# An indexed sum of a mixture-of-experts stage issued behind a branch instead of ahead of it

## The chip, the cores and the metric

The kernel runs on one core of one Trainium2 chip, in one launch. The metric is the time of one execution on the device, in microseconds (us); lower is better. The time of the kernel before is the median of three runs. All times below are us of one profiled execution unless they are marked ns, and places in it are told by the us from its start.

## The reference

Two transformer layers run one after the other on 512 tokens of width 1024, all in float32. The change lies in the last part of the second layer, a mixture of 32 experts. Two of the 32 are chosen for each token, and every expert is a small gated network:

```python
def run_block(args):
    xb, e = args
    return (jax.nn.silu(xb @ w_gate[e]) * (xb @ w_up[e])) @ w_down[e]
...
out = jnp.zeros((t, dm), jnp.float32).at[stok].add(y_sorted * sw[:, None])
...
x = x + gate2 * ffn
return rms_norm_2(x, g_final)
```

So the rows of an expert are gathered by index, pass through three products (1024 to 512 twice, 512 to 1024), and are added by index into the residual `x`, which is then normalised.

## The kernel before, in words

The expert stage fills the last third of the kernel, from about 1200 us on. It works through 16 *pairs* of experts, p and p + 16, numbered 0 to 15, with 128 rows a pair. The pair's two experts are e0 and e1.

**Products.** Weights are float32 and come from DRAM by DMA (started by SP, the sync engine). A piece of 128x1024 is a *part*; a *split* (`parts`, L118) writes it as a rounded value, by ScalarE (ACT), and the remainder, by VectorE (DVE). TensorE (PE) then makes three matmuls for each product (L128, L129, L130), so each part feeds six matmuls. A pair has 24 parts. Gate and up products gather in PSUM buffers S. A silu on ACT (L1819) and a `scalar_tensor_tensor` on DVE (L1820) make `h` of them; four transposes on PE (L1832) turn it into a PSUM buffer T; ACT and DVE split that into `hh` (L171). The down product goes to two PSUM buffers G, called `py`, one for each half of the 1024 columns. e0's down product starts in `py`, e1's is added to it. G(p, e0) below is the down product of e0 of pair p.

**The end of a pair.** `scatter` multiplies the two halves of `py` into the tile `y` (L1887, DVE; there is one `y`), and GpSimd (POOL) issues an indirect DMA that adds the rows of `y` into the residual `x2_d` in DRAM (L1888). There are only two buffers G, so the first matmul of G(p + 1, e0) has to wait until `y` of pair p has been made.

**The rows of the next pair.** `rows_in` gathers them into one of two tiles `xg` (L1711, POOL), transposes them in two halves through buffers T (L1726, PE; there are two T, shared with the transposes of `h`), scales them (L1734, three columns by ACT; L1732, one by DVE), and splits them (L1736 `x0` by ACT, L1737 `x1` by POOL).

**The pause.** After pair 6 (MID is 7) `pause` prepares the weights of pair 7, makes splits ahead, and calls `overflow`, which handles pairs with more than 128 rows in a loop under `tc.If(n > 0)` (L1932 loads n, L1933 is the branch). Every engine takes this branch. In this input n is 0, and the body isn't run.

**What sets the order.** The program is written for a scheduler that plans the queues of all engines by its own estimates; each engine then runs its queue strictly in order and waits at semaphores. A statement's place in the code is only one input to that plan. The end of the stage is `sums`, which loads `x2_d` again after the last indexed sum (L1968, waiting for `self.scattered`), and `finish`, which squares these rows (L1986 on ACT, L1989 on POOL), adds the last pair and writes the output.

Of the kernel before, what the change touches and what calls it, by code (L numbers as in the profile page):

```python
# [9 lines left out]
F32 = mybir.dt.float32  # L10
# [13 lines left out]
S, D = 512, 1024  # L24
NE, CAP = 32, 128
MID = 7
# [46 lines left out]
class Kernel:  # L73
# [1797 lines left out]
    def experts(self, h, hn_d, x2_d, loaded):  # L1871
        nc = self.nc
        last = NE // 2 - 1
        with self.pool("mo") as wk:
            first, last_x, there = self.first_rows(x2_d, wk)

            def rest():
                self.rows_scaled(1, h, hn_d, last_x)
                self.router_rest(there, last_x, wk)

            self.later = [4, rest]

            def scatter(py, row):
                y = wk.tile([128, D], F32, name="y", bufs=1)
                for half in range(2):
                    c = slice(half * 512, half * 512 + 512)
                    nc.vector.tensor_mul(y[:, c], py[half], self.g2[:, c])  # L1887
                self.scattered = nc.gpsimd.indirect_dma_start(  # L1888
                    out=x2_d, out_offset=bass.IndirectOffsetOnAxis(ap=row, axis=0), in_=y, in_offset=None,
                    bounds_check=S - 1, oob_is_err=False, compute_op=OP.add)  # L1890

            def pieces(p):
                return self.expert_pieces(p), self.expert_pieces(p + 16)

            def job(p):
                def between(rest):
                    if p < last:
                        return []
                    w, self.xs = self.sums(x2_d, rest)
                    return w  # L1900

                def done(py):
                    if p < last:
                        scatter(py, self.ti[:, p:p + 1])
                    else:
                        self.finish(py, wk)

                there = p == MID + 1
                return (pieces(p), lambda: first if p == 0 else self.rows_in(self.ti[:, p:p + 1], self.xg[p % 2], hn_d, wk, there),
                        [self.tw[:, e, p:p + 1] for e in range(2)], between, done)  # L1910

            def pause():

                self.gather(self.ti[:, MID + 1:MID + 2], self.xg[(MID + 1) % 2], hn_d)
                i = self.nraw % len(self.raws)
                raws, n = [r for r in self.raws[i:] + self.raws[:i] if r not in self.spare], 10
                self.raws, self.nraw, self.nparts = raws, 0, 0
                loaded = [self.load(w) for w in self.in_order(MID)[2:][:n]]
                ready = [self.parts(loaded[i // 2][:, i % 2 * 2:i % 2 * 2 + 2]) for i in range(2)]
                places, nparts = self.w_places, self.nparts  # L1920
                self.raws, self.w_places = self.spare, places[-1:]
                self.overflow(last, pieces, scatter, hn_d, wk)
                self.raws, self.nraw = raws[n:] + self.spare + raws[:n], 0
                self.w_places, self.nparts = places, nparts
                return loaded, ready

            self.pairs([job(p) for p in range(last + 1)], wk, loaded, MID, pause)

    def overflow(self, last, pieces, scatter, hn_d, wk):

        nc, tc = self.nc, self.tc
        n = nc.values_load(self.over[0:1, 0:1], min_val=0, max_val=7)  # L1932
        with tc.If(n > 0):  # L1933
            with tc.For_i(0, n, 1) as i:
                p = nc.values_load(self.over[0:1, bass.ds(i + 8, 1)], min_val=0, max_val=last)
                sl = wk.tile([128, 8], F32, name="osl", bufs=1)
                oj = wk.tile([128, 1], F32, name="oj", bufs=1)
                nc.vector.tensor_copy(oj, self.overj[:, bass.ds(i, 1)])
                nc.vector.tensor_scalar(sl, self.slot, oj, None, op0=OP.subtract)
                ti = wk.tile([128, 16], I32, name="oti", bufs=1)  # L1940
                tw = wk.tile([128, 2, 16], F32, name="otw", bufs=1)
                R = self.xg[MID % 2].bitcast(BF)[:, 0:1024].rearrange("p (i s) -> p i s", i=8)
                self.slot_tokens(sl, ti, R)
                self.slot_weights(tw, R)
                t1 = wk.tile([128, 1], I32, name="ot1", bufs=1)
                w1 = wk.tile([128, 2, 1], F32, name="ow1", bufs=1)
                nc.vector.tensor_copy(t1, ti[:, bass.ds(p, 1)])
                nc.vector.tensor_copy(w1, tw[:, :, bass.ds(p, 1)])
                rows = wk.tile([128, D], F32, name="y", bufs=1)
                self.pairs([(pieces(p), lambda: self.rows_in(t1, rows, hn_d, wk), [w1[:, 0], w1[:, 1]],  # L1950
                             lambda rest: [], lambda py: scatter(py, t1))], wk)

    def sums(self, x2_d, rest):

# [152 lines left out]
```

## Time and profile before

| | |
|---|---|
| median of 3 runs | 1790.49 us (1790.27 to 1791.97) |
| the profiled execution | 1795.8 us |
| its span | 1794.0 us |
| granted TensorE clock, mean | 0.988 of full speed |
| busy: PE, DVE, ACT, POOL | 96%, 77%, 64%, 26% of the span |
| L118 splits on ACT / on DVE | 353.8 + 127.7 us / 421.9 + 151.2 us |
| idle PE put down to the branch of L1933 | 5.2 us |

The profile is one execution, taken apart by engine. A busy share is an average over the span. An instruction's row has its start, its duration, its engine, its line, the tile that it writes and those that it reads, and in brackets the idle time of its engine just before it and what ended that. An engine with a q behind its name is the engine's sequencer, where branches and semaphores are handled. Matmuls overlap, so their durations add up to more than the distance between their starts.

### The profile page before, as it was taken

To read this page: it belongs to the slowest core of one execution; us is meant where nothing else is said; L and a number is where in the kernel's file an instruction comes from. 1 tells how busy PE (TensorE), PEld (TensorE's weight loads), DVE (VectorE), ACT (ScalarE), POOL (GpSimd) and SP (SyncE) were. 2 spreads that over 40 slices of the span, in tenths; PEclk is the share of its full clock that TensorE was granted. 3 is DMA by queue.
4 is the path that set the end of the run, shared out by engine and by line. 5 is a ranking of instruction groups with operands and counts; after the bars stand their busy time and mean duration, and the time that the engine had idled before them with its cause. 6 is when DMAs were issued, how large, how long until landed. Compare 5 with 4: busy or idle time off the path is not lost. (4 is left out here: it accounts for less than half of the span.)

```text
span 1794.0 us, 24961 instructions
## 1 busy us (share of the span) xinstructions
PE 1722.5 (96%) x8996; PEld 1414.4 (79%) x8996; DVE 1385.7 (77%) x2028; ACT 1149.6 (64%) x1814; POOL 461.2 (26%) x428
## 2 busy tenths in 40 slices
PE   6999999998999999999999999979999989999996
PEld 3878977887898888888978888757877767787874
DVE  4758788887687474747756877879999979999997
ACT  4646765764555343435555765568888868888886
POOL 2114326435032333333313300111212112121113
PEclk9999999998999999999999999989999999999998
DMA  9543204217446655554432224669999999999954
GB/s 344 172 130 106 78 30 160 87 60 245 149 152 210 201 184 192 187 188 159 141 95 71 71 67 165 233 203 366 366 360 366 327 323 381 374 367 365 371 209 168
DMA packets 234912, 377.71 MB, mean 211 GB/s; under 512 B 11817, under 2 KB 102565, under 8 KB 234784
## 3 DMA queue, kind: packets, MB, share of 16 engines
q1 hardware_dynamic: 223904, 348.22, 56.5%
q0 software_dynamic: 10880, 27.85, 5.2%
q8 instruction: 72, 1.18, 0.3%
q14 instruction: 56, 0.46, 0.1%
HBM read 366.64 MB, written 20.73 MB: 216 GB/s over the span
## 5 line engine op out<-in xcount | busy, mean ns | idle before, releaser
L118 ACT ACTIVATE w<-raw 128x1024 fp32r<-128x1024 f32 (+2 forms) x350 | 353.8, 1017 | 298.4 <-PE G L129 230.5
L118 DVE TENSOR_TENSOR w<-raw,w 128x1024 fp32r<-128x1024 f32 (+2 forms) x350 | 421.9, 1225 | 115.6 <-ACT w L118 113.8
L128 PE MATMUL G<-u,w 128*128 128x512 f32 (+1 forms) x688 | 265.5, 387 | 3.2 <-DVE mo L1090 1.3
L129 PE MATMUL G<-u,w 128*128 128x512 f32 (+1 forms) x688 | 264.4, 385 | 2.0 <-DVE u L922 1.1
L130 PE MATMUL G<-u,w 128*128 128x512 f32 (+1 forms) x688 | 264.7, 386 | 0.6 <-DVE w L118 0.6
L129 PE MATMUL S<-w,x 128*128 128x512 f32 x504 | 200.9, 399 | 0.8 <-DVE w L118 0.8
L128 PE MATMUL S<-w,x 128*128 128x512 f32 x504 | 196.2, 395 | 5.4 <-PEq L1933 5.2
L130 PE MATMUL S<-w,x 128*128 128x512 f32 x504 | 198.2, 393 | 0.0
L118 DVE TENSOR_TENSOR w<-rawa,w 128x1024 fp32r<-128x1024 f32 x122 | 151.2, 1271 | 15.4 <-ACT w L118 15.3
L128 PEld LDWEIGHTS G<-u,w 128*128 128x128 f32 x688 | 129.8, 189 | 30.4 <-issue 2.8
L129 PEld LDWEIGHTS G<-u,w 128*128 128x128 f32 x688 | 129.8, 189 | 27.9 <-DVE u L922 1.6
L118 ACT ACTIVATE w<-rawa 128x1024 fp32r<-128x1024 f32 x122 | 127.7, 1059 | 36.7 <-PE S L130 23.0
L130 PEld LDWEIGHTS G<-u,w 128*128 128x128 f32 x688 | 129.9, 189 | 26.3 <-DVE w L118 1.8
L406 POOL TENSOR_TENSOR acc<-acc,araw 128x512 f32<-128x512 f32 x60 | 87.6, 1479 | 236.8 <-ACT araw L404 236.6
L128 PEld LDWEIGHTS S<-w,x 128*128 128x128 f32 x504 | 95.7, 190 | 27.2 <-issue 5.7
L129 PE MATMUL G<-hid,w 128*128 128x512 f32 (+1 forms) x320 | 111.1, 347 | 1.2 <-DVE hid L1131 1.2
L129 PEld LDWEIGHTS S<-w,x 128*128 128x128 f32 x504 | 95.7, 190 | 20.3 <-DVE w L118 1.1
L130 PE MATMUL G<-hid,w 128*128 128x512 f32 (+1 forms) x320 | 111.3, 348 | 0.0
L130 PEld LDWEIGHTS S<-w,x 128*128 128x128 f32 x504 | 95.7, 190 | 19.7 <-DVE x L1773 0.3
L128 PE MATMUL G<-hid,w 128*128 128x512 f32 (+1 forms) x320 | 110.8, 347 | 0.0
L129 PE MATMUL G<-w,hh 128*128 128x512 f32 x248 | 100.7, 406 | 2.3 <-DVE w L118 0.9
L1737 POOL TENSOR_TENSOR x<-xg,x 128x512 fp32r<-128x512 f32 x30 | 44.9, 1498 | 218.9 <-ACT x L1736 218.9
(652 smaller groups left out, 4028.8 us busy)
## 6 DMA issues: line engine op xcount, KB each, us to landing
raw<-in_mlp_w_dram SPq DMA_DIRECT2D x36, 1024.0 KB, 5.5
raw<-in_w_in_dram SPq DMA_DIRECT2D x33, 1024.0 KB, 5.4
raw<-in_w_expert_up_dram SPq DMA_DIRECT2D x28, 1024.0 KB, 9.6
raw<-in_w_expert_gate_dram SPq DMA_DIRECT2D x27, 1024.0 KB, 9.2
raw<-in_w_expert_down_dram SPq DMA_DIRECT2D x27, 1024.0 KB, 8.1
araw<-in_w_ada_dram SPq DMA_DIRECT2D x96, 256.0 KB, 3.7
rawa<-in_w_expert_gate_dram SPq DMA_DIRECT2D x21, 1024.0 KB, 9.5
rawa<-in_w_expert_up_dram SPq DMA_DIRECT2D x20, 1024.0 KB, 8.5
```

Source lines behind the costliest of these rows:

```text
L118: ins = nc.scalar.activation(r[0], v, AF.Copy), nc.vector.tensor_sub(r[1], v, r[0])
L128: first = nc.tensor.matmul(ps, lhs[0], rhs[0], start=start, stop=False)
L129: nc.tensor.matmul(ps, lhs[0], rhs[1], start=False, stop=False)
L130: self.behind = nc.tensor.matmul(ps, lhs[1], rhs[0], start=False, stop=stop)
L406: nc.gpsimd.tensor_add(x, x, raw)
L1737: nc.gpsimd.tensor_sub(x[1][:, s], y[:, s], x[0][:, s])
```

## The change

`scatter` gets two arguments. `held` is true for pair 6 alone: then `y` is made as before, but the indexed sum isn't issued; `pause` issues it (`add`) behind the call of `overflow`. `pause` asks for one split ahead of `overflow` rather than two. In the body of the loop the rows go into `self.xg[MID % 2]` rather than a tile `y`, as `y` now holds pair 6's result over the loop. No instruction that runs with n = 0 is added or taken away: 15 indexed sums and 30 halves of `y` are there as before. Lines behind the change move by 1, 8 or 9: L1887 is now L1888, L1888 is L1896, L1933 is L1942, L1968 is L1977, L1986 is L1995.

```diff
-            def scatter(py, row):
-                y = wk.tile([128, D], F32, name="y", bufs=1)
+            def scatter(py, row, y=None, held=False):
+                if y is None:
+                    y = wk.tile([128, D], F32, name="y", bufs=1)
                 for half in range(2):
                     c = slice(half * 512, half * 512 + 512)
-                    nc.vector.tensor_mul(y[:, c], py[half], self.g2[:, c])
+                    ins = nc.vector.tensor_mul(y[:, c], py[half], self.g2[:, c])
+                if held:
+
+                    self.held = y, row
+                else:
+                    add(y, row)
+
+            def add(y, row):
                 self.scattered = nc.gpsimd.indirect_dma_start(
                     out=x2_d, out_offset=bass.IndirectOffsetOnAxis(ap=row, axis=0), in_=y, in_offset=None,
                     bounds_check=S - 1, oob_is_err=False, compute_op=OP.add)
...
                     if p < last:
-                        scatter(py, self.ti[:, p:p + 1])
+                        scatter(py, self.ti[:, p:p + 1], held=p + 1 == MID)
...
-                ready = [self.parts(loaded[i // 2][:, i % 2 * 2:i % 2 * 2 + 2]) for i in range(2)]
+                ready = [self.parts(loaded[0][:, 0:2])]
...
                 self.overflow(last, pieces, scatter, hn_d, wk)
                 self.raws, self.nraw = raws[n:] + self.spare + raws[:n], 0
                 self.w_places, self.nparts = places, nparts
+                add(*self.held)
                 return loaded, ready
...
-                rows = wk.tile([128, D], F32, name="y", bufs=1)
+                rows = self.xg[MID % 2]
                 self.pairs([(pieces(p), lambda: self.rows_in(t1, rows, hn_d, wk), [w1[:, 0], w1[:, 1]],
-                             lambda rest: [], lambda py: scatter(py, t1))], wk)
+                             lambda rest: [], lambda py: scatter(py, t1, rows))], wk)
```

The scheduler's queues differ in more than this. Three places of them follow, before and with the change.

**POOL at the pause.** The rows run from the last split of the rows of pair 7 to the gather of pair 8; the rows left out are the body of the loop. Before:

```order
L1737 TENSOR_TENSOR x_13926<-xg_11557,x_13925 128x512 x2
L1888 DMA x_d<-y,ti 512x1024
L1932 TENSOR_LOAD over
L1933 COMPARE_AND_BRANCH
...
L1933 ISA
L1933 UNCONDITIONAL_BRANCH
L1711 DMA xg_11557<-hn_d,ti 128x1024
```

Now:

```order
L1737 TENSOR_TENSOR x_13926<-xg_11557,x_13925 128x512 x2
L1941 TENSOR_LOAD over
L1942 COMPARE_AND_BRANCH
...
L1942 ISA
L1942 UNCONDITIONAL_BRANCH
L1896 DMA x_d<-y,ti 512x1024
L1711 DMA xg_11557<-hn_d,ti 128x1024
```

The indexed sum of pair 6 stands behind the branch, next to the gather. On PE, ACT, DVE and SP the rows ahead of the branch stand in the order that they had: the second split asked for there (and a third) is still made ahead of the branch.

**DVE around G(14, e0).** The rows `y<-G` are pair 13's result; `hh` and the rows behind it are what G(14, e0) and the rows of pair 15 need. Before:

```order
L1887 TENSOR_TENSOR y<-G,g_11351 128x512
L118 TENSOR_TENSOR w_16706<-raw_16693,w_16705 128x1024
L118 TENSOR_TENSOR w<-raw_16715,w 128x1024
L1887 TENSOR_TENSOR y<-G,g_11351 128x512
...
L118 TENSOR_TENSOR w<-rawa,w 128x1024
L171 TENSOR_TENSOR hh_16788<-T,hh_16787 128x512
L1732 TENSOR_SCALAR xg_11557<-T,gain_11126,mods_131 128x128
L118 TENSOR_TENSOR w_16826<-rawa,w_16825 128x1024
L118 TENSOR_TENSOR w_16839<-rawa,w_16838 128x1024
L118 TENSOR_TENSOR w_16849<-rawa,w_16848 128x1024
L118 TENSOR_TENSOR w<-rawa,w 128x1024
L1732 TENSOR_SCALAR xg_11557<-T,gain_11126,mods_131 128x128
```

Now:

```order
L118 TENSOR_TENSOR w<-rawa,w 128x1024
L171 TENSOR_TENSOR hh_16786<-T,hh_16785 128x512
L1732 TENSOR_SCALAR xg_11557<-T,gain_11126,mods_131 128x128
L118 TENSOR_TENSOR w_16824<-rawa,w_16823 128x1024
L1732 TENSOR_SCALAR xg_11557<-T,gain_11126,mods_131 128x128
L1888 TENSOR_TENSOR y<-G,g_11351 128x512 x2
L118 TENSOR_TENSOR w_16837<-rawa,w_16836 128x1024
```

Both halves of `y` have moved from between the splits of the pair's gate product to a place behind the second `xg`, 17 rows later for the first half. On PE the second four transposes of `xg` (L1726) have moved with it: they stood among the matmuls of G(14, e0) and now stand right ahead of them, and the first row of G(14, e0) now waits for DVE's `y`. On ACT the second three `xg` (L1734) stand right behind the first `x0` (L1736) rather than three splits later. Pair 12's `y`, in front of G(13, e0), has moved in the same way, with two splits rather than one between the two `xg`. Pair 11's two halves stand two rows ahead of the `hh` of G(12, e0), with one split between. The halves of pairs 9 and 10 stand two or three rows later than before, eight rows or more ahead of `hh`; those of pairs 7 and 8 have not moved.

**DVE behind G(14, e1).** `y` is pair 14's result, the last one that goes through an indexed sum; the last row is the `h` of (15, e0). Before:

```order
L118 TENSOR_TENSOR w_17015<-p_17012,w_17014 128x1024
L1887 TENSOR_TENSOR y<-G,g_11351 128x512
L118 TENSOR_TENSOR w_17025<-p_17012,w_17024 128x1024
L118 TENSOR_TENSOR w<-p_17034,w 128x1024
L1887 TENSOR_TENSOR y<-G,g_11351 128x512
L118 TENSOR_TENSOR w_17046<-p_17034,w_17045 128x1024
L118 TENSOR_TENSOR w_17062<-raw_17059,w_17061 128x1024
L118 TENSOR_TENSOR w_17072<-raw_17059,w_17071 128x1024
L118 TENSOR_TENSOR w<-raw_17081,w 128x1024
L1820 SCALAR_TENSOR_TENSOR h<-S,tw,h 128x512
```

Now:

```order
L118 TENSOR_TENSOR w_17013<-p_17010,w_17012 128x1024
L118 TENSOR_TENSOR w_17023<-p_17010,w_17022 128x1024
L118 TENSOR_TENSOR w<-p_17032,w 128x1024
L118 TENSOR_TENSOR w_17044<-p_17032,w_17043 128x1024
L118 TENSOR_TENSOR w_17060<-raw_17057,w_17059 128x1024
L118 TENSOR_TENSOR w_17070<-raw_17057,w_17069 128x1024
L118 TENSOR_TENSOR w<-raw_17079,w 128x1024
L1888 TENSOR_TENSOR y<-G,g_11351 128x512 x2
L1820 SCALAR_TENSOR_TENSOR h<-S,tw,h 128x512
```

The second half, which the indexed sum waits for, has moved behind four more splits. POOL's queue behind it is the same as before: the indexed sum, two weight loads, `g_final`, the four loads of `x2_d`, the last gather. On ACT the first square of `finish` has moved behind the last `hh` (`x`, L171).

## Rows read from the trace of the kernel before

**Rows 1.** Busy time by stretch: stretch, us; PE, PEld, DVE, ACT, POOL; clock; DMA.
```profile
1470.00:1530.00 60.00, 59.44 (x272) 47.31 (x271) 55.80 (x54) 50.74 (x64) 11.91 (x7) 1.00 1.04 382
```

**Rows 2.** Waits from 1470 to 1760: us in total, times, longest us.
```profile
ACT w L118 <- PE S L130: 30.7, 97, 0.5
PEld G L130 <- DVE hh L171: 5.3, 16, 0.4
```

**Rows 3.** Line L1933, the branch: ns shortest/median/longest, start of the first and last.
```profile
L1933 PEldq COMPARE_BRANCH  x1: 7982/7982/7982, 1451.3 to 1451.3; - x1
L1933 ACTq COMPARE_BRANCH  x1: 50/50/50, 1453.7 to 1453.7; - x1
```

**Rows 4.** Order of time, PE, around the pause: start, us, instruction, idle before.
```profile
1454.12 0.40 PE L130 MATMUL G<-w,hh 128*128 128x512 f32 x1
1459.76 0.76 PE L128 MATMUL S<-w,x 128*128 128x512 f32 x1 [5.25 <-PEq L1933]
...
1465.02 0.41 PE L128 MATMUL S<-w,x 128*128 128x512 f32 x1
```

**Rows 5.** Order of time, POOL, around the pause.
```profile
1438.72 1.64 POOL L1737 TENSOR_TENSOR x<-xg,x 128x512 fp32r<-128x512 f32 x1 [4.42 <-ACT x L1736]
1456.89 1.56 POOL L1888 DMA_INDIRECT x_d<-y,ti  x1 [16.52 <-DVEq L1933]
1460.23 1.06 POOL L1711 DMA_INDIRECT xg<-hn_d,ti  x1 [1.77 <-PEq L1933]
```

**Rows 6.** Order of time, DVE, from 1709 to 1732, around G(14, e0).
```profile
1711.46 0.68 DVE L1887 TENSOR_TENSOR y<-G,g 128x512 f32<-128x512 f32 x1
...
1723.61 1.23 DVE L118 TENSOR_TENSOR w<-rawa,w 128x1024 fp32r<-128x1024 f32 x1
1724.75 0.68 DVE L171 TENSOR_TENSOR hh<-T,hh 128x512 fp32r<-128x512 f32 x1
1725.35 0.40 DVE L1732 TENSOR_SCALAR xg<-T,gain,mods 128x128 f32<-128x128 f32 x1
1726.09 1.23 DVE L118 TENSOR_TENSOR w<-rawa,w 128x1024 fp32r<-128x1024 f32 x1 [0.33 <-ACT w L118]
```

**Rows 7.** Order of time, PE, at the start of G(14, e0).
```profile
1724.35 0.40 PE L130 MATMUL S<-w,x 128*128 128x512 f32 x1
...
1724.59 0.39 PE L128 MATMUL G<-w,hh 128*128 128x512 f32 x1
...
1729.10 0.60 PE L1726 MATMUL T<-ident,xg 128*128 128x128 f32 x4
```

**Rows 8.** Order of time, ACT, around G(14, e0).
```profile
1724.98 1.07 ACT L118 ACTIVATE w<-rawa 128x1024 fp32r<-128x1024 f32 x1
1725.93 0.61 ACT L1819 ACTIVATE h<-S 128x512 f32<-128x512 f32 x1
1726.41 0.65 ACT L1736 ACTIVATE x<-xg 128x512 fp32r<-128x512 f32 x1
1726.93 3.21 ACT L118 ACTIVATE w<-rawa 128x1024 fp32r<-128x1024 f32 x3
1730.05 1.14 ACT L1734 ACTIVATE xg<-T,mods,gain 128x128 f32<-128x128 f32 x3
```

**Rows 9.** Order of time, PE, after another idle time, in an earlier stage.
```profile
427.76 0.79 PE L129 MATMUL G<-kT,w 128*128 128x512 f32 x1 [2.29 <-DVE kT L171]
```

**Rows 10.** PE by stretch there: stretch, us; PE busy; clock; DMA share, GB/s.
```profile
428.00:432.00 4.00, 4.00 (x9) 0.50 0.62 204
```

**Rows 11.** Order of time, DVE and POOL, behind pair 14.
```profile
1750.11 0.68 DVE L1887 TENSOR_TENSOR y<-G,g 128x512 f32<-128x512 f32 x1
...
1758.07 2.12 POOL L1968 DMA_DIRECT2D rawa<-x_d  x4 [2.48 <-DMA x_d<-y,ti]
```

**Rows 12.** Order of time, ACT, at the end.
```profile
1768.53 1.06 ACT L1986 ACTIVATE y<-rawa 128x1024 f32<-128x1024 f32 x1 [0.42 <-DMA rawa<-x_d]
...
1776.31 0.30 ACT L205 ACTIVATE ss<-ss,eps 128x4 f32<-128x4 f32 x1
```

## The prediction

> **What bounds the kernel now.** I read busy time by stretch first: which engine is full where the change acts? From 1470 to 1530, just behind the pause, PE is busy 59.44 of 60 us at full clock, and the DMA engines are full too [rows 1]. Which of the two leads is told by the waits: ACT's splits wait for PE to free their buffers, 97 times, never over 0.5 us, and none of the longer waits of PE, ACT or DVE in that list is for a weight load [rows 2]. So PE leads, and a stop of PE there moves the rest of the stage by its full length. The one long stop of PE in the stage is the pause itself: 5.25 us idle [rows 4]. Order of time on DVE, PE and ACT around one later pair [rows 6 to 8], then on POOL, DVE and ACT at the end [rows 11, 12], show what the moved instructions lie beside.
>
> **The pause: no gain.** The stop is charged to PE's own sequencer: PE's branch lasts 7982 ns from 1451.3, ACT's 50 ns [rows 3]. PE's branch begins 5.6 us before POOL's indexed sum is issued at 1456.89 [rows 5], and PE starts again at 1459.76 [rows 4]. What the change alters for certain is POOL: it was done with pair 7's rows at 1440.4 and stood 16.52 us until pair 6's `y` [rows 5]; it can now take its branch then. The sum itself still needs `y`, so it starts at about 1457 as before, ahead of a gather that waits for PE anyway (until 1460.23, [rows 5]). The queue is past one instruction of 1.56 us, hidden by that wait. The second split isn't moved at all by the scheduler. So I cost the pause at 0; the bounds are 0 and a gain of 5.25 us plus what the clock loses behind the stop. That loss: the 12 matmuls from 1459.76 to 1465.02 take 5.26 us [rows 4], where one takes 0.23 to 0.24 at full clock (1724.35 to 1724.59, [rows 7]), 12 of them 2.8; the loss is 2.4. Together 7.7 us. The Trainium skill (Advanced Engine Details and Errata, Control Flow Timing) gives a compare-and-branch about 108 ns; ACT's 50 ns is of that kind and PE's 7982 ns is not, so by the page PE would be held by something else, which could be what the change moves. That is the first rival.
>
> **The moved products of later pairs.** The scheduler has put `y` of pairs 9 to 14 later in DVE's queue. `y` frees the two buffers G, and the next pair's first G matmul waits for it. Before, pair 13's first half was made at 1711.46 [rows 6], 13 us ahead of G(14, e0) at 1724.59 [rows 7]: hidden. Its cover was that place in the queue, and it is gone.
>
> *G(14, e0).* DVE now reaches `y` only behind the second `xg`, and that needs ACT's second three `xg`. ACT's chain up to there stays: a split at 1724.98, the silu at 1725.93, `x0` at 1726.41, done with its turn at 1726.93 [rows 8]. The silu can't come sooner by much, since it reads the S group whose last matmul starts at 1724.35 and takes 0.40 [rows 7]. The three `xg`, now next, take 1.14 [rows 8]: 1728.07. DVE's `xg` takes 0.40, `y` 0.68 [rows 6]; with 0.1 for the hand-overs that is 1729.3. PE could have begun at 1724.59 plus 0.44 for the four transposes that now stand ahead (0.11 each, an estimate: 0.60 for four with the overlap of the last, [rows 7]; this work is moved, not added): 1725.03. **The stop is 4.2 us.** The second half, 0.6 us later, is needed only 12 matmuls on, and is hidden.
>
> *G(13, e0).* The same chain; its two splits between the `xg` are both done before ACT's silu, and `hh` comes a part sooner, so it ends about 0.4 sooner: 3.8 us. The least that either can be is the silu (0.48 to the next start), `x0` (0.52), three `xg` (1.14), `xg` (0.40) and `y` (0.68) behind the last S matmul's end at 1724.75, 3.2 in all, or 1728.0 against 1725.0: 3.0 us. The most is 4.5, with another 0.3 of waiting for an ACT split [rows 6].
>
> *The clock behind them.* The stop of 5.25 us was followed by 2.4 us lost. The nearest on the other side, 2.29 us idle in an earlier stage [rows 9], was followed by a stretch at a granted clock of 0.50, which is 1.2 GHz [rows 10]; 4 us at that clock lose 2.0. Stops of 3 to 4 us lie between two that both lost it, so I take 2.4 for each; bounds 0 and 3.
>
> *G(12, e0).* Both halves of pair 11's `y` lie ahead of the last split and of `hh`. PE waits for `hh` now already (5.3 us over 16 times, [rows 2]), so nothing absorbs it except what DVE gains by not having made `y` earlier, at most 0.2: 2 x 0.6 (the distance from one such start to the next, 1724.75 to 1725.35 for `hh`, of the same length [rows 6]) less 0.2 is 1.0. Bounds 0.6 and 1.3. *G(11, e0)* and *G(10, e0)*: eight rows lie between; 0.3 for both, bounds 0 and 0.6. Pairs 7 and 8: 0.
>
> **The end.** Pair 14's second half, made at 1750.11 [rows 11], has moved behind four more splits of 1.14 (1723.61 to 1724.75, [rows 6]): 4.5 us. POOL's queue behind it moves along: the indexed sum, two weight loads, `g_final` and the loads of `x2_d`, which are already waiting 2.48 us for the sum to land [rows 11]. ACT's first square is already waiting 0.42 us for these loads [rows 12], so it would start at 1773.0 rather than 1768.53. ACT does two other things first that used to come behind it (some 1.5 us), and has 1776.31 - 1768.53 = 7.8 us of work from there [rows 12], less those 1.5: 1773.0 + 6.3 = 1779.3, 3.0 later. I take 3.0, bounds 0 (the loads land sooner, with less beside them) and 4.5.
>
> **The sum.** 0 + 0.3 + 1.0 + (3.8 + 2.4) + (4.2 + 2.4) + 3.0 = 17.1 us. On the profiled execution's own time, 1795.8, that is 1812.9; the median of the runs shown is 5.3 below that execution, so the forecast for it is 1790.5 + 17.1 = **1807.6 us**. All lower bounds together: 0 + 0 + 0.6 + 3.0 + 3.0 + 0 = 6.6, or 1797.1. All upper ones: 0.6 + 1.3 + 2 x (4.5 + 3) + 4.5 = 21.4, or 1811.9.
>
> **The rivals.**
>
> *PE's stop belongs to POOL.* If PE's branch can't end before POOL's, the change ends it early and gives back up to 7.7. For it: PE starts 2.6 us behind POOL's sum, a branch is short on ACT. Against: PE's branch is charged to nothing else, and ACT passed its own at 1453.7 with POOL still waiting [rows 3, 5]. The later stops stay: 17.1 - 7.7 = 9.4, 1799.9 us. Chance 0.07.
>
> *The other side: the pause outweighs the stops.* The same mechanism at the pause, worth 7.7, decides once the later stops sum to less than that; at their lower bounds they sum to 6.6, without a loss of clock and with the end hidden. Then 1790.5 - 1.1 = 1789.4 us, and the little between is within the measurement. Against: it needs both of the unlikely ends. Chance 0.04.
>
> *The stops are short of the clock.* All as forecast, but PE keeps its full clock: 17.1 - 4.8 = 12.3, 1802.8 us. For it: no stop of PE of 3 to 4 us is in this stage before. Against: the shorter one of 2.29 lost it [rows 9, 10]. Chance 0.24.
>
> *The moved rows cost next to nothing.* If DVE's `y` were reached as soon as before because the splits ahead of it, no longer behind `y`, all ran sooner, only the end would be left: 0 to 3 us, about 1792. Against: `y` is behind an `xg` that reads the S group's successor on ACT, and no split's haste changes that. That the change does nothing at all falls here. Chance 0.05.
>
> **How the numbers follow.** The forecast has 0.60, the four rivals 0.07, 0.04, 0.24 and 0.05. A measurement can tell about 0.2%, 3.6 us, from no change. The range runs from the sum of the lower bounds, which takes in the first and third rival, to just above that of the upper ones: 1797 to 1812. Beyond it I leave the second and fourth rival and some 0.08 for more than all upper bounds. Slower: 0.60 + 0.07 + 0.24, less 0.02 for lengths below their bounds, 0.89. Same: 0.05 from the fourth, 0.02 from the second and half of the 0.02 just taken, 0.08. Faster: the rest, 0.03.
>
> **What the profile of the changed kernel would show.** Right: POOL's branch near 1441 and the indexed sum behind it near 1457; PE's idle time at the branch still 5 us; two stops of PE of 3 to 4.5 us, put down to DVE `y`, in front of G(13, e0) and G(14, e0) near 1691 and 1732, each followed by about 12 matmuls 0.43 apart; about 1 us more waiting for `hh` a pair earlier; ACT's first square waiting some 2 us for the loads of `x2_d`. Wrong: an idle PE at the branch of under 3 us, or no wait of PE for `y` at all; if these waits are there and the total is much less than 12 us, something behind them gave time back, and DMA, which runs ahead while PE stands, would be the first to look at.

## The result, and the profile after

| | before | after |
|---|---|---|
| median, beside each other on one chip | 1791.23 us (6 runs, 1790.14 to 1793.61) | 1808.72 us (6 runs, 1804.65 to 1813.16) |
| the profiled execution | 1795.8 us | 1807.51 us |
| its span | 1794.0 us | 1805.8 us |
| granted TensorE clock, mean | 0.988 | 0.987 |
| busy: PE, DVE, ACT, POOL | 96%, 77%, 64%, 26% | 96%, 77%, 64%, 25% |

The change is slower: after over before is 1.0098, with a 95% interval from 1.008 to 1.0116. That is 17.5 us, where 17.1 was forecast for the median of 1790.49. The busy shares tell nothing of it; the waits do. Waits of PE after, from 1470 to the end (us in total, times, longest us):

```profile
PE G L128 <- ACT x L1736: 7.2, 2, 4.0
PE G L128 <- ACT w L118: 3.1, 1, 3.1
PE T L1726 <- DVE hh L171: 0.7, 1, 0.7
PE G L129 <- DVE w L118: 0.6, 2, 0.4
```

The first row is two stops in front of a first matmul of G. Order of time on PE after, at G(13, e0) and at G(14, e0):

```profile
1689.98 0.77 PE L128 MATMUL G<-w,hh 128*128 128x512 f32 x1 [3.96 <-ACT x L1736]
1690.55 0.63 PE L129 MATMUL G<-w,hh 128*128 128x512 f32 x1
1690.98 0.63 PE L130 MATMUL G<-w,hh 128*128 128x512 f32 x1
...
1728.33 0.66 PE L1726 MATMUL T<-ident,xg 128*128 128x128 f32 x4 [0.74 <-DVE hh L171]
1732.20 0.47 PE L128 MATMUL G<-w,hh 128*128 128x512 f32 x1 [3.21 <-ACT x L1736]
```

And order of time on DVE after, around the same two places:

```profile
1688.83 0.41 DVE L1732 TENSOR_SCALAR xg<-T,gain,mods 128x128 f32<-128x128 f32 x1 [0.89 <-ACT xg L1734]
1689.16 1.28 DVE L1888 TENSOR_TENSOR y<-G,g 128x512 f32<-128x512 f32 x2
...
1731.05 0.41 DVE L1732 TENSOR_SCALAR xg<-T,gain,mods 128x128 f32<-128x128 f32 x1 [0.89 <-ACT xg L1734]
1731.37 1.28 DVE L1888 TENSOR_TENSOR y<-G,g 128x512 f32<-128x512 f32 x2
```

The wait is put down to ACT's `x`, but what PE waits for is `y`: two halves take 1.28, so the first ends some 0.68 after its start [rows 6], at 1689.84 and 1732.05, and PE starts 0.14 and 0.15 later. `y` itself stands behind an `xg` that waited 0.89 for ACT.

Behind each stop the clock was at its lower level, 1.2 GHz (0.50), and came back. PE by stretch after (stretch, us; PE busy, PEld, DVE, ACT, POOL; clock; DMA share, GB/s):

```profile
1691.00:1695.00 4.00, 4.00 (x11) 3.13 (x10) 0.99 (x1) 1.06 (x1) 1.85 (x2) 0.50 1.04 315
1695.00:1699.00 4.00, 4.00 (x18) 3.23 (x17) 2.45 (x3) 2.81 (x3) 0.00 (x0) 0.95 0.52 104
...
1733.00:1736.00 3.00, 3.00 (x9) 2.33 (x8) 0.42 (x1) 1.06 (x1) 2.05 (x2) 0.50 0.25 26
```

At the pause, POOL takes its branch early, as the change intends, and issues the sum when it did before. Line L1942, the branch (ns shortest/median/longest, start of the first and last):

```profile
L1942 POOLq COMPARE_BRANCH  x1: 61/61/61, 1438.0 to 1438.0; - x1
L1942 PEldq COMPARE_BRANCH  x1: 4075/4075/4075, 1450.0 to 1450.0; - x1
...
L1942 DVEq COMPARE_BRANCH  x1: 72/72/72, 1453.9 to 1453.9; - x1
```

Order of time after, PE and then POOL, around it:

```profile
1452.86 0.39 PE L130 MATMUL G<-w,hh 128*128 128x512 f32 x1
1455.54 0.47 PE L128 MATMUL S<-w,x 128*128 128x512 f32 x1 [2.30 <-DVEq L1942]
...
1455.62 1.57 POOL L1896 DMA_INDIRECT x_d<-y,ti  x1 [16.52 <-DVEq L1942]
1457.49 1.28 POOL L1711 DMA_INDIRECT xg<-hn_d,ti  x1 [0.31 <-issue]
```

PE stood 2.30 us here rather than 5.25 [rows 4]. Whether the change did that is the first question for the experiments. At the end, order of time after on DVE, POOL and ACT:

```profile
1763.46 1.28 DVE L1888 TENSOR_TENSOR y<-G,g 128x512 f32<-128x512 f32 x2
...
1765.02 1.55 POOL L1896 DMA_INDIRECT x_d<-y,ti  x1 [29.81 <-DVE y L1888]
...
1771.61 2.22 POOL L1977 DMA_DIRECT2D rawa<-x_d  x4 [2.83 <-issue]
...
1781.45 1.06 ACT L1995 ACTIVATE y<-rawa 128x1024 f32<-128x1024 f32 x1 [2.83 <-issue]
...
1787.79 0.30 ACT L205 ACTIVATE ss<-ss,eps 128x4 f32<-128x4 f32 x1
```

The chain of work that ended last (start, us, what) runs through these loads:

```profile
1771.61 7.00 DMA rawa<-x_d
1778.61 2.75 issue
1786.61 1.16 ACT y L1995 x2
```

The profile names nothing for the two waits of 2.83 ("issue"), but the semaphores' own records in the trace do: the sum had landed at 1771.08, POOL's loads start at 1771.61, the first of them had landed at 1781.30, and ACT's square starts 0.15 later.

### The profile page after: what moved, and what is told of

Read it like the earlier page. It is cut to its first block, busy times and chain, and to the rows that moved or that the text cites. A ratio compares the mean times of both kernels' runs of the same rounds, so it can differ in the third digit from the quotient of the medians.

```text
span 1805.8 us, 24961 instructions
## 1 busy us (share of the span) xinstructions
PE 1725.4 (96%) x8996; PEld 1416.5 (78%) x8996; DVE 1388.2 (77%) x2028; ACT 1151.4 (64%) x1814; POOL 458.6 (25%) x428
```

## The experiments

**My theory:** the cost isn't at the pause. It comes from the rows of `y` that the scheduler moved on DVE (pairs 9 to 14), each term at its own place. **Rivals:** the sum behind the branch costs or gains something by itself; or the stops cost only their length, not the clock behind them.

One thing shows without a run. Two parts of the change could act with n = 0, the held sum and the one split, and only the first reaches the queues. With the held sum but two splits ahead of the pause, all queues of the built kernel, with the semaphores that they wait for, are those of the change; with one split alone, they are those of before. What the kernels below take apart is therefore the held sum.

**`y` of pairs 12 and 13 late, in the kernel before.** The pause stays as it was.

```diff
+                    ins = nc.vector.tensor_scalar(y[:, i], src, a, b, op0=OP.mult, op1=OP.add)
+                    if half:
+                        for late in self.late:
+                            self.order(late, ins)
+                        self.late = []
...
+                    ins = nc.vector.tensor_mul(y[:, c], py[half], self.g2[:, c])
+                    if p in LATE:
+                        self.late.append(ins)
```

Expected: 

> The kernel before, with the y of pairs 12 and 13 alone tied behind the second xg of the next rows but one, as the change has them; the pause is untouched. Theory (two stops of 3.2 to 4.2 us and a loss of clock of 1.6 to 2.4 us behind each): 10 to 13 us slower than before. Rival (the stops are there but the clock costs nothing): 7 to 8 us slower. Rival (the loss sits in pairs 9 to 11 and at the end): under 4 us slower.

Measured: 1805.30 us (5 runs), ratio 1.0072 (1.0058 to 1.0086), about 13 us; both rivals, of at most 8 us, fall. Waits of PE in it:

```profile
PE G L134 <- ACT x L1746: 6.8, 2, 3.6
PE S L134 <- PEq L1949: 3.4, 1, 3.4
```

The same two stops arise with the pause untouched (second row: its stop is 3.4 us here).

**`y` of pair 14 late, in the kernel before.** The same tie, to a place behind seven splits.

```diff
+        for q in getattr(self, 'late7', []):
+            if not q[0]:
+                self.order(q[1], ins[1])
+            q[0] -= 1
...
+                    if p in LATE7:
+                        self.late7.append([6, ins])
```

Expected: 

> The kernel before, with the y of pair 14 alone tied behind seven splits, as the change has it. Theory (the last indexed sum 4.5 us later, of which 3.0 reach the end): 2 to 4.5 us slower than before. Rival (the loads of x2_d are hidden by the weight loads beside them): within 1 us of before.

Measured: 1795.12 us (7 runs), ratio 1.0026 (1.0014 to 1.0038), 4.7 us by the ratio and 3.5 by the medians (before: 1791.65), so the rival of hidden loads falls. Together the two kernels carry 0.98% of cost, as the whole change does; each of the two has an interval of more than 0.1% to either side, and neither has the late `y` of pairs 9 to 11, so that the sums agree to the digit is luck. This kernel's pause, unchanged, also bears on who holds PE there. PE and POOL in order of time:

```profile
1453.77 0.40 PE L136 MATMUL G<-w,hh 128*128 128x512 f32 x1
1456.46 0.47 PE L134 MATMUL S<-w,x 128*128 128x512 f32 x1 [2.29 <-DVEq L1949]
...
1456.54 1.56 POOL L1904 DMA_INDIRECT x_d<-y,ti  x1 [16.51 <-DVEq L1949]
```

PE went on before POOL issued the sum, and POOL's branch comes behind the sum here. So this stop doesn't belong to POOL. It is a short one, though; in a second profile of before (below), where PE stood 3.6 us, PE's branch ended at 1455.0, just behind POOL's, which began at 1454.6, and that looks like the rival. What holds PE in a long stop is left to a trace further down.

**The same stops, filled.** The kernel with pairs 12 and 13 late, with 12 matmuls of ones into an unused PSUM buffer in each stop. They add nothing to the output.

```diff
+            if half and self.late:
+                self.order(self.gfirst, self.filler(FILL, turn, self.ps("O", 1)))
```

Expected: 

> As the run with the y of pairs 12 and 13 late, with 12 matmuls of constants on PE in each of the two stops, into a PSUM buffer that nobody reads (about 2.6 us of the 3.2 to 4); they leave the output alone. Theory (the clock behind a stop costs 1.6 to 2.4 us each): 3 to 5 us faster than that run, no matmuls 0.43 us apart behind the stops. Rival (the clock doesn't matter to the time): the same time within 1 us, or up to 1 us slower.

Measured: 1800.44 us (5 runs), ratio 1.0049 (1.0035 to 1.0063): 4.9 us less than unfilled by the medians, with `y` as late as before. PE in order of time:

```profile
1685.25 2.75 PE L1682 MATMUL O<-ones_b 128*128 128x512 bf16 x12
1688.61 0.47 PE L135 MATMUL G<-w,hh 128*128 128x512 f32 x1 [0.61 <-ACT x L1749]
1688.93 0.40 PE L136 MATMUL G<-w,hh 128*128 128x512 f32 x1
```

By stretch, with the columns as above:

```profile
1688.00:1692.00 4.00, 3.39 (x16) 2.77 (x16) 1.67 (x3) 1.89 (x3) 2.88 (x2) 1.00 0.97 363
```

No matmul behind either stop is 0.43 us from the next, and the clock is 1.00. The intervals of the two ratios overlap, so the size is better read in the traces. From G(12, e1) to G(13, e0), and from G(13, e1) to G(14, e0), the first matmuls start as far apart in both kernels, to within 0.02 us: the stops are equally long. From there to the end of the block the filled kernel is 1.4 us shorter at the first stop and 2.7 at the second, 4.0 in all. So a stop costs its length and, on top, 1.4 to 2.7 us in clock. The rival that they cost their length alone falls.

**The sum behind the pause, `y` tied back.** The changed kernel, with each half of `y` of pairs 7 to 14 tied ahead of a split, where it stood before.

```diff
+        if getattr(self, 'pin', None):
+            for q in self.pin:
+                if not q[0]:
+                    self.order(ins[1], q[1])
+                q[0] -= 1
+            self.pin = [q for q in self.pin if q[0] >= 0]
```

Expected: 

> The whole change, but the halves of y of pairs 7 to 14 are tied back to where they stood in DVE's queue before (within one row); what is left of the change is pair 6's indexed sum behind the branch. Theory (the moved y carry the whole loss, the pause is worth 0): the time of before within 3 us, no wait of PE for y. Rival (PE's stop at the branch ends early when POOL has branched, as the changed kernel's branch of 4.1 us against 8.0 suggests): 3 to 7 us faster than before, with an idle PE of 2 to 3 us at the branch. Second rival (something else of the change costs, at the branch or on POOL): 4 us or more slower.

Measured: 1798.82 us (10 runs), ratio 1.0034 (1.0023 to 1.0044). Over 10 us of the cost are gone, but 6 are left: the theory's 3 us are missed. The second rival has the size, but not the place. The waits show no stop for `y`, and none for POOL, but a new kind:

```profile
PE S L135 <- PEq L1952: 3.5, 1, 3.5
PE S L135 <- ACT w L119: 2.7, 3, 0.9
PE S L136 <- DVE w L119: 0.9, 3, 0.3
```

Behind pairs 9, 11 and 13 the scheduler had swapped two splits on DVE and, on PE, put one matmul of a later part twelve places early. PE stood 0.9 us for that part's split on ACT, and 0.3 behind it for the late split on DVE. The tie alone had not restored the order.

**More ties.** Splits were now tied among each other, and each half of `y` on both sides; ACT's and DVE's queues behind the pause were then those of before, row for row.

```diff
+            self.order(ins[1], self.splits[-1][1])
...
-                if not q[0]:
-                    self.order(ins[1], q[1])
+                if q[0] < 2:
+                    self.order(*((q[1], ins[1]) if q[0] else (ins[1], q[1])))
```

Expected: 

> As the first run, with the four splits behind each pair's end tied to their order as well: every queue that runs is now row for row that of before, but for pair 6's indexed sum, which stands behind POOL's branch. Theory (the pause is worth 0; the first run's loss came from three swapped splits, 1.8 us each): within 2 us of before, and about 5 us faster than the first run. Rival (PE's stop ends early once POOL has branched): 3 to 7 us faster than before. Rival (the sum behind the branch costs at the pause): 4 us or more slower.

Beside it the kernel before ran once more as a kernel of its own. Expected: 

> The kernel before, unchanged, for a second profile of its pause. Theory (the length of PE's stop at the branch is drawn anew in each execution and the change has no part in it): an idle PE between 2 and 5.5 us, other than the 5.25 us of the first profile. Rival (the changed kernel's shorter stop is the change's work): 5 us or more again.

Measured: 1797.36 us (6 runs), ratio 1.003 (1.0017 to 1.0042) to before (1792.25), and 1791.56 (8 runs) for before again, ratio 1.0001 (0.9989 to 1.0013). Before again did as the theory said: PE stood 3.6 us at its branch, and the rival of 5 us or more falls. For the ties none of the three expectations was met: not the theory's 2 us, and the 5 us lay neither at the pause nor at a load. Waits of PE:

```profile
PE S L136 <- ACT w L119: 4.6, 5, 0.9
PE S L136 <- PEq L1953: 3.7, 1, 3.7
```

The first row is five stops, one behind each of pairs 10 to 14, that neither before nor after has. The expectation spoke of the exact order, but PE's queue was not. The first place where it differs, with the rows' numbers, in this kernel and then in before:

```
7707 L136 MATMUL S_15412<-w_15437,x0_15286 128x512
7708 L136 MATMUL S_15459<-w1_15462,x0_15286 128x512
7709 L137 MATMUL S_15412<-w_15437,x0_15286 128x512
...
7707 L128 MATMUL S_15414<-w_15439,x0_15288 128x512
...
7714 L128 MATMUL S_15461<-w1_15464,x0_15288 128x512
```

The first matmul of a later part stands six places early here, and PE didn't stop for it. Behind the five pairs that follow, it stands twelve places early, and there PE waits 0.9 us for that part's split. (The next expectation wrongly gives six places for the stops.)

This kernel also settles who holds PE in a long stop. Line L1953, the branch:

```profile
L1953 POOLq COMPARE_BRANCH  x1: 61/61/61, 1437.5 to 1437.5; - x1
L1953 PEldq COMPARE_BRANCH  x1: 6422/6422/6422, 1449.6 to 1449.6; - x1
```

POOL was through its branch 12 us before PE's began, and PE stood 3.7 us all the same: a long stop doesn't belong to POOL either.

**All orders tied.** The held sum alone. Every instruction of PE, ACT and DVE behind the pause is tied to the one ahead of it in the kernel before, from a table, so that nothing but POOL's sum has moved.

```diff
+    def settle(self):
+        for e, runs in ORDER.items():
+            made = self.made[e][-sum(n for _, n in runs):]
+            seq = [made[i + j] for i, n in runs for j in range(n)]
...
+            for x, y in zip(seq, seq[1:]):
+                self.order(y, x)
```

Expected: 

> The indexed sum of the pair in front is issued behind the pause, and every instruction of PE, ACT and DVE behind the pause is tied to the one that stands ahead of it in the kernel before, so that only POOL's indexed sum has moved (in the run with the products tied one by one, PE's queue still differed: in pairs 10 to 14 one matmul of a later part stood six places early and waited for its split, which would be the 5 us left there). My theory, the whole cost comes from rows that moved on DVE behind the pause: no stop of PE over 1 us from pair 8 to the end other than those of the kernel before; ratio 0.998 to 1.002, that is 1788 to 1795 us. Rival, the sum behind the branch costs by itself (POOL late with the gather or with the loads behind it): 3 to 7 us, ratio 1.002 to 1.004, with a new wait for POOL or for a load. Rival, the pause gives something back: 2 to 8 us faster, ratio under 0.998, with PE idle under 3 us at its branch while the kernel before run beside it has more.

Measured: 1791.95 us (12 runs), before 1791.49 (17 runs), ratio 1.0003 (0.9993 to 1.0013). All waits of PE in its trace from 1440 to 1780 (the records of most of its instructions, made in a helper, bear line L110):

```profile
PE S L110 <- DVEq L2026: 2.3, 1, 2.3
PE G L110 <- DVE w L110: 1.9, 2, 1.7
PE G L110 <- DVE x L110: 0.5, 1, 0.5
```

No stop is left but the pause and those of the end that before has too. The sum behind the branch costs and gains nothing that can be measured (the interval runs from 1.3 us less to 2.3 more); within that, all of the 17.5 us lies in rows that moved.

## Why the prediction was right

This last kernel is also the best ruler for the terms. Its trace and that of after run together to within 0.07 us up to G(10, e0), 1576.47 against 1576.46, the stop at the pause included (2.3 us in both). From there the starts of the first matmuls drift apart:

| first matmul of | all orders tied | after | apart | added by the block before | forecast |
|---|---|---|---|---|---|
| G(10, e1) | 1593.93 | 1594.10 | 0.17 | G(10, e0): 0.18 | |
| G(11, e1) | 1629.70 | 1630.40 | 0.70 | G(11, e0): 0.53 | 0.3 for both |
| G(12, e1) | 1665.47 | 1667.10 | 1.63 | G(12, e0): 0.93 | 1.0 |
| G(13, e1) | 1701.23 | 1709.50 | 8.27 | G(13, e0): 6.64 | 3.8 + 2.4 |
| G(14, e1) | 1737.00 | 1750.81 | 13.81 | G(14, e0): 5.54 | 4.2 + 2.4 |
| end of the span | 1789.04 | 1805.78 | 16.74 | the end: 2.93 | 3.0 |

The terms add up to 16.7 here, against 17.1. That this is so close is in part luck: two terms were too small by 0.4 each and one too large by 1.1.

**The pause: forecast 0, right in the sum, wrong in what the profile would show.** I expected PE to stand 5 us there still and named under 3 us as a sign of error. After shows 2.30. But the length differs from one execution to the next with the pause unchanged: 5.25 in the profile of before, 3.6 in before again, 3.4 in two kernels and 2.3 in the one with pair 14 late. With the sum behind it: 2.3, 3.5, 3.7, 2.3. The profile of before had drawn a long one; the forecast took the length of one execution for that of all. Before again had a span 5.3 us shorter than it (1788.7 against 1794.0), and half of that lay at the pause: the first matmul of G(7, e0), behind the pause, started 5.3 us sooner, 1468.86 against 1474.16, that of G(6, e1), ahead of it, 2.67 sooner, 1445.24 against 1447.91.

**Who holds PE at its branch.** The page Advanced Engine Details and Errata of the Trainium skill (Control Flow Timing) gives a compare-and-branch about 108 ns. The traces agree in kind for POOL, ACT and DVE (61, 50 and 72 ns) and not for PE (3775 to 7982 ns). From that came the rival that PE is held by POOL. The kernel with pair 14 late refutes it for a short stop and the one with more ties for a long one, and POOL's early branch in the last kernel gained nothing. (The 2.6 us that the rival gives from POOL's sum to PE's start are 2.87 by [rows 4, 5].)

**G(10) and G(11):** 0.71 rather than 0.3, a little above the upper bound of 0.6. This term was sized too low: in G(11, e0) one matmul stood 0.60 from the next rather than 0.23, the pattern of the wait for `hh` in G(12, e0). Eight rows between hid less than I took them to; the 0.3 stood on no row of its own.

**G(12, e0): forecast 1.0, measured 0.93**, by the step as put: `hh` and the split ahead of it are each later by the two `y`. One reading behind it was wrong: the 5.3 us that I took for PE's wait for `hh` are a row of PEld [rows 2], the weight loads, which overlap with matmuls; before, the first matmuls of G(12, e0) start at most 0.31 us apart. DVE after, and PE:

```profile
1647.47 1.28 DVE L1888 TENSOR_TENSOR y<-G,g 128x512 f32<-128x512 f32 x2
1648.67 1.21 DVE L118 TENSOR_TENSOR w<-p,w 128x1024 fp32r<-128x1024 f32 x1
1649.81 0.68 DVE L171 TENSOR_TENSOR hh<-T,hh 128x512 fp32r<-128x512 f32 x1
...
1649.94 0.50 PE L129 MATMUL G<-w,hh 128*128 128x512 f32 x1 [0.41 <-DVE w L118]
```

**G(13, e0):** 6.64 against 6.2. The stop row is 3.96 against 3.8; the twelve matmuls from 1689.98 on then took 5.26 us, as at the pause in before [rows 4], 2.4 too many. The remaining 0.3 has no row of its own.

**G(14, e0):** 5.54 against 6.6. The length of the stop was nearly right: the two waits make 0.74 + 3.21 = 3.95, against 4.2. (PE began G(14, e0) 4.39 later, 12.66 us apart at 1732.20 less 8.27; the 0.44 between is what the forecast put down for the four transposes that now stand ahead.) The 0.74 fell in front of the transposes, which wait for `hh` to free a buffer T; the forecast had put the whole stop behind them. The term that was mis-sized most is the clock. Only eight matmuls ran 0.43 apart here, some 1.6 us lost rather than 2.4. With pairs 12 and 13 late alone it was the other way round, 1.4 us at the first stop and 2.7 at the second, so 2.4 for each was no more than a middle value.

**The end: forecast 3.0, measured 2.9**, by the loads of `x2_d`, as forecast: ACT's first square stands 2.83 us and the chain runs through the loads. That it hits so closely is luck. The square itself came 4.1 us later (forecast 4.5), the row that the forecast ends with (L205) 2.6, and 0.3 more was lost behind it. With pair 14 late alone, the stretch from G(14, e1) to the end is 3.4 us longer than in the last kernel. PE's late weights show here as well: it stood 3.1 us for a last split of ACT, behind the square on ACT's queue.

**The rivals.** That the moved rows cost nothing, that the pause outweighs them and that the stops keep the clock all fell, the last one to the filled stops. Even so the bounds were worth giving: the clock term differed between two stops of nearly the same length.

## What to carry to other kernels

Under a scheduler, moving one instruction on an idle queue can change other queues far behind it; compare the queues first, and cost each moved row by who waits for it. To test a part alone, tie the order of every engine: each partial tie here left a new stop of its own, 5 or 6 us in all. And when PE sets the pace, add to the length of a stop of 2 to 5 us the slow matmuls behind it, here 1.2 to 2.7 us.

## What was not expected of the hardware

PE's branch was recorded at 3.8 to 8.0 us in executions of the same code ahead of it, against 50 to 72 ns on the other engines. The record isn't all idle time: in all nine traces it begins 2.8 us before PE's last matmul ahead of it does (in before at 1451.3, with that matmul at 1454.12 [rows 3, 4]). Where it was long, PE went on about 0.5 us after its end: in before at 1451.3 + 7.98 = 1459.28 against 1459.76 [rows 3, 4], and in before again likewise (1448.7 + 6.33 = 1455.0). Line L1933 in before again:

```profile
L1933 PEldq COMPARE_BRANCH  x1: 6332/6332/6332, 1448.7 to 1448.7; - x1
```

PE's first matmul behind it, in order of time:

```profile
1455.47 0.77 PE L128 MATMUL S<-w,x 128*128 128x512 f32 x1 [3.60 <-PEq L1933]
```

Where it was short, PE waited for DVE instead, and 2.3 us is then the least that was seen. After is such a case: PE's branch ended at 1450.0 + 4.08 = 1454.1, DVE's began at 1453.9, and PE went on at 1455.54. The DMA packets in the traces tell what its length goes with. In all nine, PE's branch ends 1.33 to 1.41 us after a packet of 16 KB of instructions (queue q8) has landed: at 1459.30 after 1457.89 in before, at 1455.00 after 1453.66 in before again, at 1454.11 after 1452.70 in after. That packet starts 1.4 us behind the start of PE's branch in the shortest case and 5.4 in the longest. So PE's branch seems to wait for instructions to be loaded; no run here varied that load, and what puts it off in some executions stays open.

A wait for several semaphores can bear the wrong name: ACT's `x` at both stops, where `y` on DVE came last.
